# Stick-breaking attention with its products for two query blocks at a time

## Chip, cores and metric

One core of one Trainium2 chip. The metric is device time in microseconds (us), the median of several executions. TensorE does the matrix products, VectorE and ScalarE the elementwise work, GpSimd (POOL) and SyncE (SP) issue most of the transfers.

## What is computed

Two blocks follow each other on one sequence of 1024 tokens of width 1024. The change touches one part of the first block, the stick-breaking attention: 16 heads of 64, query blocks of 128, keys up to the end of the query's own block.

```python
def stick_breaking_attention(q, k, v):
    for i in range(seq // Q_BLOCK):                 # 8 blocks of 128 queries
        ...
        z = jnp.einsum('bhqd,bhkd->bhqk', qb, kb) * inv_sqrt_d
        mask = kpos < qpos
        log_beta = jax.nn.log_sigmoid(z)
        log_1m_beta = jnp.where(mask, log_beta - z, 0.0)
        suffix = lax.cumsum(log_1m_beta, axis=3, reverse=True) - log_1m_beta
        a = jnp.where(mask, jnp.exp(log_beta + suffix), 0.0)
        outs.append(jnp.einsum('bhqk,bhkd->bhqd', a.astype(vb.dtype), vb))
```

The mask is strict: a query doesn't see its own position, so the last key of a query block has weight zero for every query of that block.

## The kernel before

The program is written as one order of instructions for each engine. A planner (class `Sched`, L58) makes this order: it keeps a clock for each engine, prices every instruction in `note` (L153) and lets side tasks (Python generators) put in their instructions when the planned clock has come to the time that they wait for. The main line is a row of projections (`run_q0`, `run_z0`, ... at L2268 on), the attention is a side task. On the chip each engine runs its list in order and waits on semaphores. All instructions are recorded in a helper, so matrix products show L249 and almost everything else L250 in the profile; it is the tile names that tell them apart: `pj` and `pv` projections (operands in a reduced fp32 format, fp32r, split in high and low parts), `z` scores, `ob` or `om`/`be` the weights, `tr` transposes, `aT` transposed weights, `o` the products with the values, `vp` the values.

Stick-breaking runs in two halves of 512 queries (`stick`, L1068). For each head pair `p` (8 of them), query block `i` (4 in a half) and head `h` there is one unit, `work`. At most three units are under way (`crew`, L1035). A unit forms the scores (`z`, L1091), sigmoid of minus and plus the scores on ScalarE (`om` and `be`, L1094), a running product from the last key backwards on VectorE (L1100), and the weights (L1102). This leaves the last key's column of `be` as it was. `turn` (L1009) transposes the weights 128 x 128 at a time on TensorE, four blocks to a PSUM bank, and ScalarE copies them to `aT`. When both heads of a query block are there, the products with the values follow (L1117): for each key block and head one product in full fp32, 64 columns of values as weights, 128 columns of `aT` moving past them. The two heads write to the two halves of the partitions. The last key block takes only 127 rows, which leaves the last key out. A PSUM bank holds the four query blocks of a half; when the third is done the gate `z` is loaded (L1126), after the fourth VectorE multiplies (L1135), and the result stays in SBUF for the output projection if at least ten big buffers are free (L1136) or goes by way of memory.

Big buffers are 34 tiles of 4 KB a partition (`N4`); a task that needs some waits in `room` (L312) until the count allows it. In `stick` a unit with over 512 keys asks for three (`om`, `be`, `aT`) and holds one until the products are done.

The output projection of the first half (`run_bo0`, L2275) begins after the first half's stick-breaking, that of the second half (`run_bo1`, L2283) after projections of the second block.

Of the kernel before, what the change touches and what calls it, by code (L numbers as in the profile page):

```python
# [12 lines left out]
ACTF = mybir.ActivationFunctionType  # L13
# [5 lines left out]
HT = 512  # L19
# [38 lines left out]
class Sched:  # L58
# [94 lines left out]
    def note(self, eng, op, out, args, extra=0.0):  # L153
        ready = self.ready
        names = [a.tensor.name for a in args]
        self.seq += 1
        start = max([self.clk[eng]] + [ready.get(n, 0.0) for n in names])
        o = out.tensor.name
        n = out.free_size()
        lat = 0.1  # L160
        if eng == "pe":
            start = max(start, self.fresh.pop(o, 0.0))
            if op == "transpose":
                d = 0.113 if self.t > 30.0 else 0.213
            elif args[0].dtype == F32R:
                d = n / 2400 if n >= 256 else n / 600
            elif args[0].dtype == BF16:
                d = n / 2400
            elif n == 1:
                d = 0.2 if self.t > 30.0 else 0.37  # L170
            else:
                d = n / 600 if args[0].free_size() == 128 else n / 1070
            d += 0.0026
        elif eng == "act":
            d = n / 1400 + 0.155 + extra
        elif eng == "dve":
            fast = op in ("tensor_scalar", "tensor_copy") and all(a.space == out.space != bass.MemoryType.PSUM
                                                                  for a in args)
            d = n / (1920 if fast else 960) + 0.06
            if op == "reciprocal":  # L180
                d += n / 192
        else:
            d = 1.05 if eng == "pool" else 0.55
            nbytes = n * out.shape[0] * 4
            t = max(self.clk["dma"], start + d) + nbytes / 360e3
            self.clk["dma"] = t
            lat = t + 1.8 - start - d
        self.clk[eng] = start + d
        for nme in names + [o]:
            self.last[nme] = self.seq, max(start + d + lat, self.last.get(nme, (0, 0.0))[1])  # L190
        ready[o] = max(ready.get(o, 0.0), start + d + lat) if eng != "pe" else start + d + lat
        if eng != "pe":
            for nme in names:
                b = self.in_bank.get(nme)
                if b is not None:
                    b[0] = max(b[0] or 0.0, start + d)
# [68 lines left out]
def tile_body(  # L265
# [14 lines left out]
    sch = Sched()  # L280
    ten, sca, vec, syn, pol = (Engine(e, n, sch, plan is None) for e, n in (
        (nc.tensor, "pe"), (nc.scalar, "act"), (nc.vector, "dve"), (nc.sync, "sp"), (nc.gpsimd, "pool")))
    acq = Engine(nc.scalar, "actq", sch, plan is None)
    mm = ten.matmul
    act = sca.activation
# [11 lines left out]
    out = out[0]  # L297
# [10 lines left out]
    def free(n=1):  # L308

        in_use[0] -= n  # L310

    def room(n, hold=0):  # L312

        while in_use[0] + n > N4:
            yield 0.4
        in_use[0] += hold

    def big(shape, dt=F32, name="b", held=False):
        in_use[0] += not held
        return s4.tile([128] + shape, dt, nm(name))  # L320

    def sml(w=HT, dt=F32, name="s"):
        return s2.tile([128, w], dt, nm(name))
# [4 lines left out]
    def bank(name="ps"):  # L328
        return sch.new_bank(lambda n: pp.tile([128, HT], F32, tag=f"bk{n}", name=nm(name)))
# [371 lines left out]
    flags = set()  # L701
# [307 lines left out]
    def turn(src, n):  # L1009

        dst = wide(n * 128, name="aT", held=True)
        for b0 in range(0, n, 4):
            b1 = min(n, b0 + 4)
            yield from sch.a_bank()
            ps = bank("tr")
            for b in range(b0, b1):
                ten.transpose(out=ps[:, (b - b0) * 128:(b - b0 + 1) * 128],
                              in_=src[:, b * 128:(b + 1) * 128], identity=ident)
            sca.copy(out=dst[:, b0 * 128:b1 * 128], in_=ps[:, 0:(b1 - b0) * 128])
        yield dst  # L1020
        return dst

    def fetched(loads, keys, need, fetch, tiles, ahead=1):

        for n, key in enumerate(keys):
            while (need(key) not in flags) or (n > ahead and keys[n - ahead - 1] not in loads["done"]):
                yield 0.5
            yield from room(tiles + (KEEP if n else 0))
            loads[key] = fetch(key)
# [38 lines left out]
    def stick(live, half, width, rho):  # L1068
        nk = (half + 1) * HT
        kv, qs = stick_in[half]  # L1070
        st = {}

        def work(p, i, h):
            yield from arrived(kv, p)
            yield from arrived(qs, p)
            n = i + 1
            w = n * 128
            kk, vt, q = kv[p][0][h], kv[p][1], qs[p][h]
            yield kk, q
            qb = q[:, :, (i % 4) * 128:(i % 4 + 1) * 128]  # L1080
            yield from room(1 if w <= HT else 3, int(w > HT))
            if w <= HT:
                both = big([2, HT], name="ob")
                om, be = both[:, 0, :], both[:, 1, :]
            else:
                om, be = big([D], name="om"), big([D], name="be")
            for c0, c1 in CUTS[n]:
                yield from sch.a_bank()
                ps = bank("z")
                o = ps[:, 0:c1 - c0]  # L1090
                mm(o, lhsT=qb[:, 0, :], rhs=kk[:, c0:c1], start=True, stop=False)  # L1091
                mm(o, lhsT=qb[:, 1, :], rhs=kk[:, c0:c1], start=False, stop=True)
                e = min(c1, w)
                act(out=om[:, c0:e], in_=ps[:, 0:e - c0], func=ACTF.Sigmoid, scale=-1.0)  # L1094
                act(out=be[:, c0:e], in_=ps[:, 0:e - c0], func=ACTF.Sigmoid)
            yield om


            rev = om[:, 0:w][:, ::-1]
            vec.tensor_tensor_scan(out=rev, data0=rev, data1=cst1["begin"][:, D - w:D][:, ::-1], initial=0.0, op0=ALU.mult,  # L1100
                                   op1=ALU.add)
            vec.tensor_tensor(out=be[:, 0:w - 1], in0=be[:, 0:w - 1], in1=om[:, 1:w], op=ALU.mult)  # L1102
            free(w > HT)
            yield be
            aT = yield from turn(be, n)
            free()
            got = st.setdefault((p, i), {})
            got[h] = aT
            if len(got) < 2:
                return  # L1110
            if p not in st:
                yield from sch.a_bank()
            if p not in st:
                st[p] = [bank("o"), 0]
            po = st[p][0]
            yield vt
            for kb in range(n):  # L1117
                r = slice(0, 127 if kb == n - 1 else 128)
                for hh in range(2):
                    mm(po[64 * hh:64 * hh + 64, (i % 4) * 128:(i % 4 + 1) * 128],  # L1120
                       lhsT=vt[r, kb * 128 + 64 * hh:kb * 128 + 64 * hh + 64],
                       rhs=got[hh][r, kb * 128:(kb + 1) * 128], start=kb == 0, stop=kb == n - 1)
            free(2 * (w > HT))
            del st[p, i]
            st[p][1] += 1
            if st[p][1] == 3 and ("z", p, half) in flags:  # L1126
                zs[p, half] = sml(name="zl")
                syn.dma_start(out=zs[p, half], in_=z_d[p, :, hs(half)])
            if st[p][1] == 4:
                o = sml(name="o")  # L1130
                z = zs.get((p, half))
                if z is None:
                    vec.tensor_copy(out=o, in_=po)
                else:
                    vec.tensor_tensor(out=o, in0=po, in1=z, op=ALU.mult)  # L1135
                if z is not None and in_use[0] + R_OB <= N4:  # L1136
                    flags.add(("oB", p, half))
                    sch.spawn(split_to(("oB", p, half), o))
                else:
                    store(o_d[p, :, hs(half)], o)  # L1140
                del kv[p], qs[p], st[p]
                free(3 + 2 * half)
                kv["done"].add(p)
                qs["done"].add(p)

        yield from crew(live, [(p, i, h) for p in range(8) for i in range(4 * half, 4 * half + 4) for h in range(2)],
                        work, width, lambda p, i, h: rho * 0.32 * (i + 1), lambda: flags.add(("stick", half)))
# [1186 lines left out]
```

## Time and profile before

| | us |
|---|---|
| median of 3 runs | 2580.68 (2580.65 to 2581.55) |
| profiled execution | 2582.41 |
| its span | 2580.6 |
| TensorE busy | 2505.5 (97%) |
| weight loads busy | 2057.5 (80%) |
| VectorE busy | 1792.8 (69%) |
| ScalarE busy | 1255.7 (49%) |
| GpSimd busy | 490.0 (19%) |

The mean granted clock of TensorE was 0.991 of its full 2.4 GHz. A group of instructions is a line, an engine and an operation with its tiles, written out<-in. A busy time is the union of the records' times, and records of TensorE overlap and have modelled ends; how often one follows the other is read from their starts.

### The profile page before, as it was taken

Reading aid. Unit: us, or ns where it says so; the run is one execution under the profiler, and the core shown is the slowest. Engines: PE = TensorE matmul, PEld = TensorE weight load, DVE = VectorE, ACT = ScalarE, POOL = GpSimd, SP = SyncE. Lnnn points to the kernel's source line nnn. Section 1 sums busy time; section 2 is a strip of 40 time slices with the busy share of each in tenths; the row PEclk is TensorE's granted clock in tenths of the full one; section 3 lists DMA queues with packets and bytes.
Section 4 is the critical chain, followed back from the end, with each engine's and each line's share of the span. In section 5 each row is a group of like instructions: output and inputs, shape, how many; then the busy total and the mean of one; then the engine's idle time right before and its main releaser. Section 6 shows DMA issues by size and latency. Waiting matters only on the chain.

```text
span 2580.6 us, 38805 instructions
## 1 busy us (share of the span) xinstructions
PE 2505.5 (97%) x13215; PEld 2057.5 (80%) x13215; DVE 1792.8 (69%) x3245; ACT 1255.7 (49%) x2529; POOL 490.0 (19%) x894
## 2 busy tenths in 40 slices
PE   7999999989999899998999999999999899999998
PEld 6888888879877677787888887888888678788887
DVE  7866666777697788986765556774666876677555
ACT  5311112555455677677664353564634634345442
POOL 0012112312101002331211321222222222221000
PEclk9999999999999999999999999999999999999999
DMA  9867869857897665775876978977886987978764
GB/s 283 264 190 201 203 214 280 235 185 249 279 274 222 204 163 157 221 192 140 250 217 160 262 209 261 260 226 220 200 237 217 237 225 235 238 225 252 226 201 130
DMA packets 541726, 570.43 MB, mean 221 GB/s; under 512 B 32910, under 2 KB 410008, under 8 KB 541528
## 3 DMA queue, kind: packets, MB, share of 16 engines
q1 hardware_dynamic: 482644, 381.99, 50.3%
q0 software_dynamic: 56528, 181.75, 25.3%
q10 hardware_dynamic: 2356, 4.21, 0.4%
q8 instruction: 104, 1.70, 0.3%
q14 instruction: 94, 0.77, 0.1%
HBM read 466.90 MB, written 186.91 MB: 253 GB/s over the span
## 4 chain that ended last, share of the span: by engine, by line
PE 65%; DVE 5%; DMA 3%; ACT 2%; issue 2%; SPq 0%; POOL 0%; DVEq 0%; ACTq 0%; POOLq 0%
PE pj L249 53%; PE o L249 4%; PE z L249 4%; PE tr L250 3%; DVE om L250 2%; PE pv L249 1%; DMA wr<-sg_d2g 1%; DVE be L250 1%; DVE wl L250 1%; DMA wr<-in_b_w_out_dram 1%; DVE ob L250 1%; DVE act L250 0%; DVE fa L250 0%; ACT om L250 0%; ACT be L250 0%
## 5 line engine op out<-in xcount | busy, mean ns | idle before, releaser
L249 PE MATMUL pj<-act,wh 128*128 128x512 f32 (+1 forms) x5680 | 1783.0, 395 | 26.2 <-DVE act L250 16.8
L249 PEld LDWEIGHTS pj<-act,wh 128*128 128x128 f32 x5680 | 1046.2, 189 | 256.8 <-DVE act L250 22.9
L249 PE MATMUL pj<-act,wl 128*128 128x512 f32 (+1 forms) x2840 | 1113.7, 392 | 0.0
L249 PEld LDWEIGHTS pj<-act,wl 128*128 128x128 f32 x2840 | 536.2, 189 | 123.1 <-DVE wl L250 1.3
L250 DVE TENSOR_TENSOR wl<-wr,wh 128x512 fp32r<-128x512 f32 x714 | 476.4, 679 | 169.7 <-ACT wh L250 156.2
L250 ACT CAST wh<-wr 128x512 fp32r<-128x512 f32 x714 | 425.8, 617 | 177.6 <-PE pj L249 41.8
L250 POOL COPY paced<-wl 128x1 f32<-128x1 f32 x256 | 114.7, 448 | 881.6 <-DVE wl L250 840.9
L250 ACT COPY aT<-tr 128x512 f32<-128x512 f32 (+3 forms) x272 | 128.7, 501 | 162.0 <-PE tr L250 159.6
L249 PE MATMUL z<-kd,qs 128*128 128x512 f32 (+2 forms) x704 | 166.4, 350 | 1.7 <-DVE o L250 0.7
L250 DVE SCALAR_TENSOR_TENSOR acc<-mw,silu_c,acc 128x512 f32<-128x512 f32 x196 | 146.5, 748 | 2.7 <-DMA mw<-in_a_mod_w_dram 0.3
L249 PEld LDWEIGHTS z<-kd,qs 128*128 128x128 f32 x704 | 113.7, 190 | 19.4 <-issue 7.2
L250 DVE TENSOR_TENSOR_SCAN om<-om,begin 128x640 f32<-128x640 f32 (+3 forms) x64 | 120.6, 1885 | 10.2 <-ACT om L250 10.2
L249 PEld LDWEIGHTS o<-aT,vp 128*64 128x64 f32 (+2 forms) x1440 | 99.9, 149 | 22.8 <-issue 14.5
L249 PE MATMUL o<-aT,vp 128*64 128x128 f32 (+2 forms) x1440 | 116.3, 280 | 0.4 <-ACT aT L250 0.4
L250 ACT COPY u<-pj 128x512 f32<-128x512 f32 x46 | 27.0, 588 | 157.8 <-PE pj L249 80.1
L250 ACT ACTIVATE p<-p,t 128x256 f32<-128x256 f32 (+7 forms) x128 | 81.3, 636 | 20.7 <-DVE t L250 20.5
L250 ACT ACTIVATE sq<-xn 128x512 f32<-128x512 f32 x48 | 30.6, 637 | 110.6 <-DVE xn L250 110.5
L250 ACT ACTIVATE om<-z 128x384 f32<-128x384 f32 (+2 forms) x128 | 69.3, 542 | 22.6 <-PE z L249 19.0
L249 PE MATMUL pj<-wh,act 128*128 128x256 f32 x448 | 79.9, 281 | 0.0
L250 PE MATMUL tr<-ident,be 128*128 128x128 f32 x416 | 61.1, 283 | 18.1 <-DVE be L250 17.7
L250 PEld LDWEIGHTS tr<-ident,be 128*128 128x128 f32 x416 | 47.3, 143 | 32.4 <-DVE be L250 20.7
L250 DVE TENSOR_TENSOR be<-be,om 128x639 f32<-128x639 f32 (+3 forms) x64 | 66.2, 1034 | 6.7 <-ACT sq L250 0.5
(252 smaller groups left out, 2757.5 us busy)
## 6 DMA issues: line engine op xcount, KB each, us to landing
wr<-in_w_in_dram SPq DMA_DIRECT2D x136, 256.0 KB
mw<-in_w_ada_dram SPq DMA_DIRECT2D x96, 256.0 KB
wr<-in_a_w_in_dram SPq DMA_DIRECT2D x80, 256.0 KB
al<-dn_d SPq DMA_DIRECT2D x77, 256.0 KB
wr<-in_w_up_dram SPq DMA_DIRECT2D x66, 256.0 KB
sw_d<-in_w_down_dram POOLq DMA_DIRECT2D x48, 352.0 KB, 5.0
wr<-in_b_w_qz_dram SPq DMA_DIRECT2D x64, 256.0 KB
qs<-q_d SPq DMA_DIRECT2D x64, 256.0 KB
```

Of the source, the lines that this page charges most:

```text
L249: return f(out, *value, **kw)
L250: return f(out=out, **kw)
```

## The change

Two neighbouring query blocks `i0` and `i0 + 1` of a head share their transposed weights: for each key block 256 columns, the first 128 of the one and the last 128 of the other query block. `turn_pair` writes them there. `pair_new` gives the place: for block pair 0 one small tile, for pair 2 one big buffer, for pairs 4 and 6 two big buffers, for each head. The unit of the first block of a pair asks for them (`room`) and the second waits until the first has begun. The products are made once for both heads and both query blocks are there: for each key block one product of 256 columns, and for the last key block, which only the second query block sees, one of 128. The last key's weight is set to zero by a new ScalarE Copy with scale 0 on one column, and the last key block takes all 128 rows. `z` is loaded after the first pair, when two query blocks are done. The planner's price for full-fp32 products is changed too: it was 128/600 us for 128 columns past full weights and 128/1070 past half-width weights, and is 0.213 and 0.108 us there, and for 256 columns 0.233 and 0.116 us.

```diff
@@ -169,7 +169,7 @@
-                d = n / 600 if args[0].free_size() == 128 else n / 1070
+                d = max(n / 1100, 0.213) if args[0].free_size() == 128 else max(n / 2200, 0.108)
@@ -1020,6 +1020,30 @@
+    def pair_tiles(i):
+
+        return (i % 8) // 2 if i < 4 else 2
+
+    def pair_new(i):
+        return [sml(name="aT")] if i == 0 else [big([2 * HT], name="aT", held=True) for _ in range(pair_tiles(i))]
+
+    def pair_block(tiles, kb, j):
+
+        return tiles[kb // 4][:, kb % 4 * 256 + 128 * j:kb % 4 * 256 + 256]
+
+    def turn_pair(src, n, tiles, j):
+
+        for b0 in range(0, n, 4):
+            b1 = min(n, b0 + 4)
+            yield from sch.a_bank()
+            ps = bank("tr")
+            for b in range(b0, b1):
+                ten.transpose(out=ps[:, (b - b0) * 128:(b - b0 + 1) * 128],
+                              in_=src[:, b * 128:(b + 1) * 128], identity=ident)
+            dst = tiles[b0 // 4].rearrange("p (k j q) -> p k j q", j=2, q=128)
+            sca.copy(out=dst[:, 0:b1 - b0, j, :], in_=ps[:, 0:(b1 - b0) * 128].rearrange("p (k q) -> p k q", q=128))
+        yield tiles
@@ -1078,7 +1102,13 @@
-            yield from room(1 if w <= HT else 3, int(w > HT))
+            i0, j = i & ~1, i % 2
+            extra = 0 if j else pair_tiles(i)
+            while j and (p, i0, h) not in st:
+                yield 0.4
+            yield from room((1 if w <= HT else 2) + extra, extra)
+            if not j:
+                st[p, i0, h] = []
@@ -1093,6 +1123,7 @@
+            act(out=be[:, w - 1:w], in_=be[:, w - 1:w], func=ACTF.Copy, scale=0.0)
             yield om
@@ -1102,11 +1133,14 @@
-            aT = yield from turn(be, n)
+            aT = st[p, i0, h]
+            if not aT:
+                aT.extend(pair_new(i0))
+            yield from turn_pair(be, n, aT, j)
             free()
-            got = st.setdefault((p, i), {})
-            got[h] = aT
-            if len(got) < 2:
+            done = st.setdefault((p, i0), [])
+            done.append((h, j))
+            if len(done) < 4:
                 return
@@ -1114,16 +1148,17 @@
-            for kb in range(n):
-                r = slice(0, 127 if kb == n - 1 else 128)
+            got = [st.pop((p, i0, hh)) for hh in range(2)]
+            for kb in range(i0 + 2):
+                j0 = int(kb > i0)
                 for hh in range(2):
-                    mm(po[64 * hh:64 * hh + 64, (i % 4) * 128:(i % 4 + 1) * 128],
-                       lhsT=vt[r, kb * 128 + 64 * hh:kb * 128 + 64 * hh + 64],
-                       rhs=got[hh][r, kb * 128:(kb + 1) * 128], start=kb == 0, stop=kb == n - 1)
-            free(2 * (w > HT))
-            del st[p, i]
-            st[p][1] += 1
-            if st[p][1] == 3 and ("z", p, half) in flags:
+                    mm(po[64 * hh:64 * hh + 64, (i0 % 4 + j0) * 128:(i0 % 4 + 2) * 128],
+                       lhsT=vt[:, kb * 128 + 64 * hh:kb * 128 + 64 * hh + 64],
+                       rhs=pair_block(got[hh], kb, j0), start=kb == 0, stop=kb > i0)
+            free(2 * pair_tiles(i0))
+            del st[p, i0]
+            st[p][1] += 2
+            if st[p][1] == 2 and ("z", p, half) in flags:
```

## Rows read from the trace of the kernel before

**Rows 1.** The page, busy us of each engine with its share of the span.
```profile
PE 2505.5 (97%) x13215; PEld 2057.5 (80%) x13215; DVE 1792.8 (69%) x3245; ACT 1255.7 (49%) x2529; POOL 490.0 (19%) x894
```

**Rows 2.** Windows: stretch, length, busy us of PE, PEld, DVE, ACT, POOL; clock; DMA.
```profile
690.00:880.00 190.00, 187.10 (x1129) 144.17 (x1127) 152.04 (x252) 107.48 (x256) 20.01 (x37) 1.00 0.86 258
880.00:1210.00 330.00, 303.34 (x2242) 252.65 (x2243) 277.80 (x332) 241.89 (x532) 67.59 (x94) 0.97 0.63 173
```

**Rows 3.** Waits of TensorE, 690 to 1210 us: total, times, longest.
```profile
PE tr L250 <- DVE be L250: 17.7, 20, 3.7
```

**Rows 4.** Lines by form: count, busy us, mean ns of one, idle before.
```profile
L249 PE MATMUL o<-aT,vp 128*64 128x128 f32 x896 | 63.3, 283 | 0.4 <-ACT aT L250 0.4
L249 PE MATMUL o<-aT,vp 127*64 127x128 f32 x256 | 26.2, 278 | 0.0
L249 PEld LDWEIGHTS o<-aT,vp 128*64 128x64 f32 x896 | 49.4, 139 | 18.1 <-issue 13.0 <-ACT ob L250 2.9 <-ACT aT L250 0.7
L249 PEld LDWEIGHTS o<-aT,vp 128*128 128x128 f32 x288 | 36.4, 191 | 2.2
```

**Rows 5.** Time line of TensorE, 863 to 865 us: start, length, operation, count.
```profile
864.41 0.66 PE L249 MATMUL o<-aT,vp 128*64 128x128 f32 x8
865.01 0.55 PE L250 MATMUL tr<-ident,ob 128*128 128x128 f32 x3
```

**Rows 6.** Time line of TensorE, 1102 to 1105 us.
```profile
1102.04 0.63 PE L249 MATMUL pj<-act,wh 128*128 128x512 f32 x2
1102.50 0.39 PE L249 MATMUL pj<-act,wl 128*128 128x512 f32 x1
1102.82 1.53 PE L249 MATMUL o<-aT,vp 128*64 128x128 f32 x24
1104.29 0.76 PE L250 MATMUL tr<-ident,be 128*128 128x128 f32 x5
```

**Rows 7.** Time line of TensorE, 1206 us: 256 columns in the reduced format.
```profile
1206.19 0.29 PE L249 MATMUL pv<-wh,act 128*128 128x256 f32 x1
1206.31 0.28 PE L249 MATMUL pv<-wl,act 128*128 128x256 f32 x1
```

**Rows 8.** Time line of TensorE, 993 us: full fp32 with 264 columns.
```profile
992.76 0.71 PE L249 MATMUL row<-row,ones 1*128 1x264 f32 x2
993.40 0.55 PE L249 MATMUL o<-aT,vp 128*64 128x128 f32 x6
```

**Rows 9.** Time line of TensorE, 40 us: full fp32 with one column.
```profile
39.75 0.95 PE L249 MATMUL sm<-ones,acc 128*128 128x1 f32 x8
40.56 0.71 PE L249 MATMUL pj<-act,wh 128*128 128x512 f32 x2
```

**Rows 10.** Lines, 690 to 1210 us: VectorE's scan and ScalarE's smallest operation.
```profile
L250 DVE TENSOR_TENSOR_SCAN om<-om,begin 128x640 f32<-128x640 f32 (+3 forms) x64 | 120.6, 1885 | 10.2 <-ACT om L250 10.2
L250 ACT ACTIVATE t<-t 128x2 f32<-128x2 f32 (+1 forms) x9 | 1.8, 199 | 0.1
```

**Rows 11.** Time line of all engines, end of the first half; idle time and releaser in brackets.
```profile
879.83 0.69 DVE L250 TENSOR_TENSOR o<-o,zl 128x512 f32<-128x512 f32 x1 [6.95 <-DMA zl<-z_d]
...
884.78 1.33 PE L250 MATMUL tr<-ident,be 128*128 128x128 f32 x5 [3.71 <-DVE be L250]
```

**Rows 12.** The chain that ended last within 866 to 900 us: start, length, what.
```profile
872.86 7.67 DMA wr<-in_b_w_out_dram
```

**Rows 13.** Tile `o`: count, ns min/median/max, first and last start.
```profile
L250 DVE TENSOR_TENSOR o<-o,zl x13: 685/692/692, 761.0 to 1209.0; 128x512 f32<-128x512 f32 x13
L250 POOL DMA_DIRECT2D o_d<-o x10: 539/542/582, 718.5 to 1154.6; - x10
...
L250 DVE COPY o<-o x3: 683/691/692, 717.5 to 997.2; 128x512 f32<-128x512 f32 x3
```

**Rows 14.** Time lines of TensorE (1205 us on) and SP's queue (1322 us on).
```profile
1206.99 1.97 PE L249 MATMUL o<-aT,vp 128*64 128x128 f32 x32
...
1325.80 7.53 SPq L250 DMA_DIRECT2D wr<-in_b_w_out_dram  x5
```

## Prediction

> **What bounds the kernel now.** I began with the busy times on the page: TensorE is busy 97% of the span [rows 1]. Busy time of TensorE is a model, so I next looked at the stretch that the change touches, stick-breaking, in two windows [rows 2]: the first half of the queries (690 to 880 us) and the second (880 to 1210 us). In the first, TensorE is busy for 187.1 of 190 us and VectorE for 152.0. In the second TensorE leaves 26.7 of 330 us unused and VectorE is busy for 277.8, 84%. Who waits for whom comes third: between 690 and 1210 us the longest wait of TensorE is for VectorE's `be`, the finished weights that are transposed next, 17.7 us in 20 pieces [rows 3]. So the first half is bound by TensorE, and time taken from it there is time gained. In the second half some of it may only lengthen the wait for VectorE. Last I went down to single products in the time line, because the price of one product decides this case.
>
> **The products, before.** For one key block the two heads' products run side by side in the two halves of the array's columns. One product of full fp32 is two records, so four records stand for one key block. There are 896 + 256 = 1152 of them [rows 4], which is 288 key blocks (8 head pairs times 1 to 8 blocks) in 64 groups, one for each pair and query block. A group of 8 records lasts 0.60 us until the next operation starts [rows 5], one of 24 lasts 1.47 us [rows 6]. The difference is 0.87 us for 16 records, 0.054 us each: 0.218 us for a key block, 0.109 us for two records side by side. What is left over, 0.60 - 8 x 0.054 = 0.165 us, is fixed for each group. Ahead of the group there is more: the last projection record starts 0.32 us before it, while two of them take 0.46 us when projections follow one another [rows 6]. That is 0.32 - 0.23 = 0.09 us. **A group thus costs 0.25 us beyond its records**, for going over to half-width columns and back.
>
> **What 256 columns cost.** The change turns 128 + 128 columns past two loads into 256 past one. Per head pair 1 + 3 + 5 + 7 = 16 key blocks go to 256 columns and 4 stay at 128. Over 8 pairs these are 128 and 32 key blocks, so 256 and 64 steps of two records side by side, instead of 576 steps of 128 columns. It saves streaming only if the 0.109 us of a step is the load of the values and not the 128 columns. No full-fp32 product of 256 columns past half-width weights stands in this trace, so I bound it. From below: a record of the reduced fp32 format with 256 columns starts 0.12 us before the next [rows 7]. From above: the two `row` records, full fp32 with 264 columns (from one partition), take 0.64 us until the next operation, 0.32 each [rows 8].
>
> Two rows point in opposite directions. Eight full-fp32 records with one moving column and a load of 128 weight columns take 0.81 us, 0.10 each [rows 9]: there the load sets the pace, and by analogy it could set it in the products. But in the products the load is of 64 columns for each head and takes 139 ns against 191 ns for 128 columns [rows 4], so it is shorter by 52 ns and the step is still 0.109 us. And the 0.64 us of `row` take apart cleanly: 0.10 us for the first load, which nothing hides [rows 9], 0.09 us for going over to half-width products behind them, and 0.45 us for two records, 0.225 us each. That is 264 columns at 0.109 us per 128 columns. I take the value in proportion to the columns, 0.218 us for a step of 256, because `row` is the only full-fp32 row with so many columns. Streaming then gains nothing: 256 x (0.218 - 2 x 0.109) = 0.
>
> The Trainium skill has a sentence for each side. FP8 and Floating Point Precision, TensorE Precision Notes, gives true fp32 four passes through the array; with two records for a product that is two passes in each, and the rows of `row` agree. Perfetto Trace Analysis, Engine Utilization, gives the low-high fp32 mode half of the array's output rate, which would be one pass for each record; by it the sum would be that of rival B below.
>
> **The sum.**
> - Groups: 64 become 32, because one group now serves two query blocks. 32 x 0.25 = 8 us of TensorE time less, 4 in each half. The first half is bound by TensorE and gives all 4. Of the second I count 2, because TensorE's spare time there is larger than the saving [rows 2] and it waits for VectorE [rows 3]; the bounds are 0 and 4.
> - Streaming: 0. Between its bounds it would be -25 us (0.12 a step) and +26 us (0.32).
> - The new one-column Copy on ScalarE, 128 of them (16 heads, 8 query blocks). The nearest row is an operation on two columns, 199 ns [rows 10], so 128 x 0.2 = 26 us of ScalarE, which is busy for 107.5 + 241.9 = 349 of the 520 us [rows 2]. It stands behind the sigmoids of its block, and the scan on VectorE, which needs `om` alone, takes 1.9 us on average meanwhile [rows 10]. I count nothing. Without that cover each block's chain would be 0.2 us longer; what queues behind it on ScalarE is the next weight split.
> - The copies out of the transposes keep number and size; only the place that they write to changes. Nothing.
> - The last group of the first half now holds two query blocks, four key blocks instead of one query block's four of 128: 3 x 0.218 us more behind the last transpose, +0.7 us. The projection of the output waits for it, so it counts. Elsewhere the products of a pair's first block now wait for the second block's weights, but nothing except the multiplication by `z` at the end of a half waits for them.
> - The load of `z` is issued one query block earlier, by SP, ahead of loads of `q` and weights. In the trace VectorE stands still for 6.95 us at 879.8 us for the last of these loads, and TensorE then waits 3.71 us [rows 11]. A gain of up to 3.7 us offers itself, but ScalarE was at that time held up until 880.5 us by a weight load of 7.67 us [rows 12], which comes next after this one. I count nothing, and -3.7 as the bound.
> - The planner's new price for a 256-column product is 256/2200 + 0.003 = 0.119 us, so 0.237 for both heads; by my reading it is 0.436, so it thinks 128 x 0.2 = 25 us of TensorE time away and lays the side work out accordingly. Projections then stand rather too early in the order than too late, which costs waiting in neither engine that I can point to: 0, with 3 us either way.
>
> Sum: -4 - 2 + 0.7 = -5.3 us, rounded to **-6 us** because the bounds on `z` and on the second half lie below. The profiled execution took 2582.41 us (span 2580.6 us), 1.7 us over the median of 2580.68. Taken from the first it gives 2576.4; for the median I forecast **2574.7 us**.
>
> **The rivals.**
> A is the forecast: columns set the price, half of the group switches are saved, 2574.7 us (2569 to 2581 with the bounds that are not streaming).
> B: the load sets the price, and a step of 256 columns takes 0.12 us. For it stand the one-column records [rows 9], against it the halved load [rows 4] and `row` [rows 8]. It would save 0.098 x 64 = 6.3 us in the first half, and 0.098 x 192 = 18.8 us in the second, of which half to all arrive: 2574.7 - 6.3 - 9.4 to 18.8 = 2550 to 2559, say 2555 us.
> C, the slower side: the pool of 34 big buffers. Two heads' pairs hold four transposed buffers in the second half until all four units are done, where each query block held two. In the trace 13 outputs were multiplied by `z` in place and 10 outputs went by way of memory, only 3 of these for lack of `z`: so at 7 of 13 ends over 24 of the 34 were in use [rows 13]. If the three units at work fall to two, the second half's 329 us (880 to 1209 us, where the last group of products ends) become 494 and end at 1374 us, 48 us after the second output projection's weights were first fetched (1325.8 us) [rows 14]. Below 117 us of lengthening it costs nothing, since nothing waits for this end before that. 2574.7 + 48 = 2623 at worst, 2600 for half of it.
> D: the order of the second half takes the rest back: its 2 us go, and VectorE's and ScalarE's extra waits take 1 to 3 us more. 2578 to 2581, say 2579 us.
>
> **How the numbers follow.** A 0.58, B 0.15, C 0.12, D 0.15. What can be told from no change is about 0.2%, 5.2 us: below 2575.5 counts as faster, above 2585.8 as slower. A straddles the lower line; I give it 0.34 faster and 0.24 same. B is faster, D is same, C is slower (0.12). Faster 0.49, same 0.39, slower 0.12. The range 2553 to 2584 takes in A with its bounds, D, and the greater part of B; C and the fast end of B are left out, somewhat under 0.2.
>
> **What would show it.** In the profile after: 640 records of this product, of them 512 with 256 columns; such records side by side start 0.21 to 0.22 us apart (A) or 0.12 us (B). 32 groups, with 0.09 us ahead and 0.165 us in each, as before. TensorE's unused time between 880 and 1210 us stays near 27 us (A) or grows by what the products gave up (D). The 128 Copies take about 0.2 us each and nobody is released by them. If C holds, the last group of the second half ends after 1325 us. I am wrong if a step of 256 columns takes clearly less than 0.21 us, if the groups' switches are not halved, or if the stretch before 690 or after 1400 us changes by more than the whole.

## The result and the profile after

| | before | after |
|---|---|---|
| median of 4 executions each, on the same chip, us | 2581.11 | 2601.80 |
| profiled execution, us (span) | 2582.41 (2580.6) | 2603.45 (2601.6) |
| mean granted clock of TensorE | 0.991 | 0.986 |

The ratio is 1.0073 with a 95% interval of 1.0051 to 1.0094: 19 us slower (0.0073 x 2581; the medians differ by 20.7), where 6 us faster was forecast. The time lies 18 us above the upper end of the range.

**The products do what was forecast.** From the page-wide list of groups by shape, then from TensorE's time line of the second half (start, duration, records, then idle time and its releaser), kernel after:

```profile
L249 PE MATMUL o<-aT,vp 128*64 128x256 f32 x512 | 65.5, 397 | 0.0
L249 PE MATMUL o<-aT,vp 128*64 128x128 f32 x128 | 13.3, 277 | 0.0
L250 ACT ACTIVATE be<-be 128x1 f32<-128x1 f32 x64 | 13.0, 203 | 2.0
L250 ACT ACTIVATE ob<-ob 128x1 f32<-128x1 f32 x64 | 13.0, 203 | 2.0
```
```profile
1103.28 2.60 PE L249 MATMUL o<-aT,vp 128*64 128x256 f32 x24
1105.80 1.08 PE L249 MATMUL z<-kd,qs 128*128 128x512 f32 x4
...
1126.53 3.46 PE L249 MATMUL o<-aT,vp 128*64 128x256 f32 x32
1129.92 0.33 PE L250 MATMUL tr<-ident,be 128*128 128x128 f32 x1
```

512 and 128 records, as counted beforehand against 1152 in [rows 4]. The group of 32 lasts 3.39 us until the next operation starts, that of 24 lasts 2.52; the difference of 0.87 us is eight records of 256 columns, four steps of 0.2175 us. Twice a step of 128 columns is 0.218 [rows 5, 6]. What is left of the larger group is 3.39 - 14 x 0.2175 - 2 x 0.109 = 0.13 us, not far from the 0.165 us of a group before. The Copy takes 203 ns, as assumed.

**What went wrong stands in the windows.** Columns as in [rows 2]; first the two stretches of [rows 2], then the end of the first half and the main line's last wait for an attention, kernel after:

```profile
690.00:880.00 190.00, 182.11 (x982) 139.60 (x982) 152.43 (x254) 118.82 (x325) 21.07 (x39) 1.00 0.88 261
880.00:1210.00 330.00, 296.32 (x1771) 237.95 (x1769) 255.14 (x335) 227.88 (x537) 63.33 (x91) 0.94 0.59 163
860.00:940.00 80.00, 65.63 (x350) 50.03 (x349) 51.43 (x61) 46.60 (x118) 1.76 (x4) 0.87 0.46 136
1840.00:1920.00 80.00, 76.09 (x366) 62.68 (x365) 47.11 (x94) 41.75 (x70) 20.15 (x37) 0.98 0.88 218
```
The last two for the kernel before:
```profile
860.00:940.00 80.00, 72.19 (x516) 58.67 (x517) 65.98 (x67) 57.62 (x129) 3.25 (x6) 0.96 0.62 184
1840.00:1920.00 80.00, 80.00 (x375) 65.66 (x374) 50.46 (x92) 35.73 (x61) 18.68 (x37) 1.00 0.87 235
```

In the second half (880 to 1210 us) TensorE's unused time grows from 26.7 to 33.7 us and its clock falls from 0.97 to 0.94. VectorE, 84% busy there before, does 22.7 us less in the same stretch, and ScalarE 14.0 less. So none of these engines became busier there: units of work come later. The stretch then runs on. The groups of VectorE's multiplication by `z` and of the second attention's output statistics, by tile (duration ns, then first and last start), after and then before:

```profile
L250 DVE TENSOR_TENSOR o<-o,zl x14: 685/691/692, 767.7 to 1311.8; 128x512 f32<-128x512 f32 x14
L250 ACT ACTIVATE sq<-o x8: 600/604/605, 1332.2 to 1886.4; 128x512 f32<-128x512 f32 x8
```
```profile
L250 DVE TENSOR_TENSOR o<-o,zl x13: 685/692/692, 761.0 to 1209.0; 128x512 f32<-128x512 f32 x13
L250 ACT ACTIVATE sq<-o x8: 602/604/607, 1278.9 to 1856.5; 128x512 f32<-128x512 f32 x8
```

The second half's stick-breaking ends at 1311.8 us instead of 1209.0, 103 us later, and what follows it, the second block's attention, at 1886.4 instead of 1856.5. The main line falls behind along the way. Counted in projection records, the 3600th starts 0.1 us later than before (925 us), the 4800th 18.6 us (1395 us), the 6600th 25.7 us (1883 us), the 9450th 21.3 us (2556 us). The 2400th (591 us), ahead of all that the change touches, is already 3.2 us late in this execution, so a few us of such counts say nothing. The line thus loses ground at two places, up to 1400 us and around 1885 us. On the way to the first it seemed to gain: at 1210 us the projections were 42.6 us ahead, because TensorE had not done the attention's share, and that share came after.

### The profile page after: what moved, and what is told of

Same layout as the page of the kernel before. It is cut to its first block, busy times and chain, and to the rows that moved or that the text cites. A ratio compares the mean times of both kernels' runs of the same rounds, so it can differ in the third digit from the quotient of the medians.

```text
span 2601.6 us, 37805 instructions
## 1 busy us (share of the span) xinstructions
PE 2508.6 (96%) x12703; PEld 2048.0 (79%) x12703; DVE 1791.9 (69%) x3244; ACT 1287.6 (49%) x2665; POOL 488.9 (19%) x892
## 4 chain that ended last, share of the span: by engine, by line
PE 51%; DVE 4%; ACT 2%; DMA 1%; issue 1%; SPq 0%; DVEq 0%; ACTq 0%
PE pj L249 42%; PE o L249 3%; PE z L249 2%; PE tr L250 2%; PE pv L249 1%; DVE om L250 1%; DMA wr<-in_w_up_dram 1%; DVE p L250 1%; DVE wl L250 1%; ACT om L250 0%; ACT be L250 0%; DVE fa L250 0%; DVE t L250 0%; DMA wr<-sg_d0g 0%; DMA wr<-sg_d3a 0%
## 5 line engine op out<-in xcount | busy, mean ns | idle before, releaser
L250 DVE TENSOR_TENSOR_SCAN om<-om,begin 128x640 f32<-128x640 f32 (+3 forms) x64 | 120.6, 1885 | 26.3 <-ACT om L250 26.2
L249 PE MATMUL o<-aT,vp 128*64 128x256 f32 (+2 forms) x928 | 109.4, 343 | 0.3 <-ACT aT L250 0.2
L249 PEld LDWEIGHTS o<-aT,vp 128*64 128x64 f32 (+1 forms) x928 | 81.2, 156 | 32.5 <-issue 7.3
```

The source lines that it names most:

```text
L249: return f(out, *value, **kw)
L250: return f(out=out, **kw)
```

## Experiments: which half, which part

All are compared with the kernel before on the same chip; "end" is the last multiplication by `z` of the second half.

**e1, e2: the planner's price alone.** In e1 the kernel before has the new price line, in e2 the changed kernel the old one.

```diff
-                d = n / 600 if args[0].free_size() == 128 else n / 1070
+                d = max(n / 1100, 0.213) if args[0].free_size() == 128 else max(n / 2200, 0.108)
```


> The kernel before with nothing but the planner's new price for full-fp32 products (0.213 and 0.108 us at 128 columns in place of 128/600 and 128/1070); no product changes. Pool theory (the second half's units and fetches wait for big buffers, because two heads' pairs hold four of the 34): 2581 +-5 us, end of the second half's stick-breaking at 1209 +-15 us. Price theory (the planner's wrong prices disturb the order): about 2595 to 2602 us. Structure theory (products that wait for four units): 2581 us.

> The changed kernel with the old price line in the planner (a 256-column product past half-width weights at 256/1070 = 0.239 us, close to the 0.21 to 0.22 us that the trace of after shows). Pool theory: still slow, 2602 +-8 us, the second half's last products after 1290 us. Price theory: 2576 +-6 us. Structure theory: 2602 us.

e1: 2586.21 us, ratio 1.0009 (1.0000 to 1.0018). e2: 2599.57 us, 1.0064 (1.0049 to 1.0079), end 1312.0. By the medians the price is worth 2 or 3 us; without it the changed kernel still loses 0.64%, so it is not the cause.

**e3, e4: pairs in one half only.** The changed lines are kept for one half, the old ones for the other; e4 has `PAIRED = (1,)`. Both have the new price.

```diff
+    PAIRED = (0,)
...
+            if half in PAIRED:
```


> Pairs in the first half alone (blocks 0 to 3, where a pair holds at most one big buffer a head); the second half as before, without the Copy; new price. Pool theory: the first half's gain stays and the second half loses nothing: 2573 to 2578 us, last products near 1209 us. Price theory: 2590 to 2600 us. Structure theory (half of the pairs, half of the loss): about 2590 us.

> Pairs in the second half alone (blocks 4 to 7, two big buffers a head); the first half as before; new price. Pool theory: all of the loss and none of the first half's gain: 2602 to 2612 us, last products after 1290 us. Price theory: 2590 to 2600 us. Structure theory: about 2590 us.

e3: 2583.81 us, 1.0001 (0.9991 to 1.0011), end 1210.0. e4: 2593.44 us, 1.0039 (1.0024 to 1.0054), end 1280.5. The first half gains nothing, although its groups are halved; the second half alone loses 10 us. Together they lose 19: the two are not a sum. Both miss what the theory of the buffer pool alone expected (2573 to 2578 and 2602 to 2612 us).

**e9: without the Copy.** The changed kernel; the last key's weight is not set to zero, so that part of the computation is left out.

```diff
-            act(out=be[:, w - 1:w], in_=be[:, w - 1:w], func=ACTF.Copy, scale=0.0)
```


> The changed kernel without the one-column Copy on ScalarE (the last key's weight is then not set to zero; 128 operations of 203 ns, 26 us of ScalarE, are left out). Theory that the Copy lengthens every unit's chain: the second half ends 10 us or more earlier and the time falls to 2590 us or less. Pool theory: 2601 +-4 us, end of the second half near 1310 us.

2595.66 us, 1.0046 (1.0031 to 1.0061), end 1272.7. The Copy is worth about 6 us by the medians, with intervals that overlap, and 39 us of the end. The time lies between the two theories' ranges.

## Experiments: why the first half gives nothing

**e10, e11: a wait moved.** Late in the main line, projections of the feed-forward (`run_up0`, pieces 0 to `M_BR`) stand before the wait for the second attention's second half. The edit puts one more piece in front; e10 has the pairs in the first half only, e11 is the kernel before.

```diff
-M_BR = 5
-M_WO = 6
+M_BR = 6
+M_WO = 7
```


> Pairs in the first half alone, and one more step of the up projection put ahead of the wait for the second attention (M_BR 6, M_WO 7 in place of 5 and 6). Gate theory (in e3 the main line is 5.8 us ahead at 1800 us and loses 7.4 us at 1865 us, where it waits for the end of the second attention): that wait goes, what TensorE loses between 1840 and 1920 us falls from 8.2 to about 1 us, and the time is 2574 to 2580 us. If the saved time was lost elsewhere: 2584 us as e3.

> The kernel before with the same step ahead of the same wait: control for e10. Before loses 0.9 us between 1840 and 1920 us, so nothing is to be had there: 2581 to 2588 us by the gate theory. If it gains as much as e10, the gain of e10 is not that of the pairs.

**e10 takes 2577.93 us, ratio 0.9977 (0.9967 to 0.9987): faster than both kernels.** e11 takes 2595.8 us, 1.0045 (1.0030 to 1.0060), so it is not the edit by itself. This control missed its range (2581 to 2588 us), and why it is slow stays open: at the 6900th projection (1953 us) it is level with the kernel before, at the 8100th (2252 us) 12.9 us behind, where e10 loses nothing. The window of the wait, e3 and then e10:

```profile
1840.00:1920.00 80.00, 76.09 (x343) 62.03 (x342) 49.95 (x91) 35.18 (x60) 16.42 (x31) 0.96 0.84 212
```
```profile
1840.00:1920.00 80.00, 80.00 (x374) 65.67 (x373) 51.73 (x95) 39.99 (x66) 18.96 (x34) 1.00 0.87 231
```

In e3 TensorE came to this point 5.8 us earlier than before (the 6300th projection), but the attention's last statistics were taken at 1861.1 us instead of 1856.5. TensorE waited ahead of two small products of these statistics, and its granted clock was half for 6.8 us from 1863.8 us on. Its waits in this window in e3 (total, times, longest):

```profile
PE rb L250 <- DVE t L250: 2.3, 1, 2.3
PE sm L250 <- ACT sq L250: 1.4, 1, 1.4
```

With the up to 3.4 us that half clock costs in 6.8, all the gain was gone. Before, this wait does not exist. With the wait a piece later TensorE is busy for all 80 us at full clock, and the gain arrives.

**e5, e6: the wait at the first half's end moved.** Two more pieces of the `z` projection ahead of the wait for the first half's stick-breaking, with the pairs in the first half (e5) and in the kernel before (e6).

```diff
-N_Z = 2
+N_Z = 4
```


> Pairs in the first half alone, and two more of the gate projections (48 products of 512 columns, 11 us of TensorE) put ahead of the wait for the first half's end (N_Z 4 in place of 2). Gate theory (the first half's TensorE time was saved, about 4 us, but the main line then waits at the end of stick-breaking's first half for a chain through ScalarE and VectorE that ends no earlier): 2574 to 2579 us, and what TensorE loses between 860 and 940 us falls from 23 to about 15 us. Theory that the pairs themselves slow the units at the boundary: 2584 us as in e3, the loss moves with them.

> The kernel before with the same two projections ahead of the wait (N_Z 4), nothing else: control for e5. Gate theory: there the main line and the chain end together (878 and 880 us), so moving 11 us of work ahead of the wait delays what comes after it: 2581 to 2588 us. If it is faster by as much as e5, the gain of e5 is not that of the pairs.

e5: 2585.89 us, 1.0008 (0.9998 to 1.0017). e6: 2591.82 us, 1.0030 (1.0019 to 1.0040). With this order the pairs of the first half are worth 6 us, e5 against e6, but the order itself costs more than that, and both lie above their ranges (e5 2574 to 2579, e6 2581 to 2588 us). In e5 the projections were 20.8 us ahead at 998 us and 0.4 us behind at 1064 us: the time was given back at the next wait.

## Experiments: why the second half is late

**e13: held, but not paired.** The kernel before; in the second half the products of two neighbouring query blocks wait for all four units and are then made with 128 columns, block after block.

```diff
+            ii = i & ~1 if half else i
...
-            if len(got) < 2:
+            if len(got) < (4 if half else 2):
...
+            for iq in range(ii, ii + 1 + half):
...
-            free(2 * (w > HT))
+            free(2 * (1 + half) * (w > HT))
```


> The kernel before; only in the second half the products of two neighbouring query blocks wait until all four units (two query blocks, two heads) are done, and are then made one query block after the other with 128 columns, as before; the four transposed buffers are held until then. z is loaded when the first two query blocks are done. No 256-column product, no Copy, the old price. Theory (holding): the second half's last multiplication by z comes at 1250 to 1320 us instead of 1209, TensorE's unused time grows in 940 to 1080 us and around 1880 us, and the time is 2589 to 2600 us, near the kernel with pairs in the second half alone (2593). Rival (the wide products themselves, their order of writing, the Copy): the end stays within 10 us of 1209 and the time within 4 us of before.

2603.07 us, 1.0073 (1.0058 to 1.0088), end 1245.5.

```profile
L250 DVE TENSOR_TENSOR o<-o,zl x13: 684/691/693, 762.9 to 1245.5; 128x512 f32<-128x512 f32 x13
```

No wide product, no Copy, no new price, and the time of the changed kernel. The time is 3 us over the theory's range and the end 4.5 us below it; the rival (4 us, an end within 10 us) is out. Making the products wait for four units, and holding the transposed weights until then, is enough for a loss of 19 us. With wide products, the Copy and the new price on top (e4) it is 10 us: together these give some back. Not all of the 19 us need be the holding's own. In its profiled execution e13 falls 14 us behind between the 2400th and the 6900th projection (591 and 1953 us) and 9 us more by the 8100th, in the stretch where e11 loses 12.5 us with no holding at all. So a rival was not tested and may hold for a part: that a changed order costs time by itself, as it does in e6 and e11 (8 and 12 us without a pair), though not in e17.

**e8: two buffers fewer, nothing held.**

```diff
-N4 = 34
+N4 = 32
```


> The kernel before with 32 big buffers in place of 34, nothing else: what two buffers fewer cost by themselves. Pool theory: the second half's end goes from 1209 to 1270 us or later, 2590 to 2602 us. Structure theory: 2581 to 2586 us, end near 1209 us.

2626.94 us, 1.0165 (1.0150 to 1.0180), end 1259.8. That is 25 us over the upper end of the range. The window of the late wait shows where it goes:

```profile
1840.00:1920.00 80.00, 48.06 (x244) 42.17 (x243) 42.73 (x125) 40.21 (x71) 11.18 (x23) 0.77 0.52 129
```

TensorE stands idle for 32 of these 80 us. The pool is so tight that two of 34 buffers delay the second half's end by 51 us. But the pool serves the whole program: the second attention's last statistics come at 1913.1 us, 57 us later, and at the 6300th projection, before that wait, TensorE is 26.8 us ahead of the kernel before. So e8 shows that buffers are short, not what their lack in stick-breaking alone costs.

**e7, e12: one big buffer for each head of a pair,** with key blocks from the fifth on in small tiles; e7 in the changed kernel, e12 with pairs in the second half only.

```diff
-        return (i % 8) // 2 if i < 4 else 2
+        return int(i > 0)
...
+        return t + [sml(name="aT") for _ in range(1 if i == 0 else max(0, i // 2 - 1))]
```


> The changed kernel, but the transposed weights of key blocks 4 to 7 in small tiles from the other pool: a head's pair holds one big buffer where it held two, as many as a query block held before; one ScalarE copy more where a bank is split in two. Pool theory: the end of the second half's stick-breaking comes back from 1312 to 1215 +-20 us and the time to 2586 +-6 us (the loss at the first half's end stays). Structure theory: end at 1290 to 1312 us, 2600 us.

> Pairs in the second half alone with one big buffer a head and small tiles for key blocks 4 to 7: e4 (2593.4 us, end at 1280 us) with fewer big buffers. Pool theory: the end comes back to 1209 to 1240 us and the time to 2582 to 2588 us. Structure theory (products and buffers that wait for four units, however large): 2591 to 2596 us, end near 1280 us.

e7: 2592.64 us, 1.0032 (1.0019 to 1.0045), end 1262.7. e12: 2592.51 us, 1.0038 (1.0026 to 1.0049), end 1260.4. Half of the delay of the end goes and 9 us of the time in e7; against e4, e12 gains nothing that can be told. With half of the big buffers for each later pair, the theory of the pool expected the end at 1195 to 1235 (e7) and 1209 to 1240 us (e12), and both missed it.

**e16, e17, e18: the loads.** Loads of a head pair's keys and values, and of its queries, need buffers of their own (three and two) and wait in `fetched` (L1023) until `KEEP` = 7 more are free. Issues of the keys' loads from 880 us on, by tile (the last two numbers are first and last start): after, before, e13.

```profile
L250 SPq DMA_DIRECT2D kd<-k_d x12: 338/440/3739, 965.5 to 1210.0; - x12
```
```profile
L250 SPq DMA_DIRECT2D kd<-k_d x12: 319/338/455, 932.9 to 1109.3; - x12
```
```profile
L250 SPq DMA_DIRECT2D kd<-k_d x12: 320/403/655, 946.7 to 1169.6; - x12
```

The third head pair's keys are asked for 33 us later and the last pair's 101 us later, about the delay of the end. The edit lets the second half's loads go with three more buffers free (`keep` is 3 there); e16 is the changed kernel, e17 the kernel before, e18 the kernel of e7.

```diff
-            yield from room(tiles + (KEEP if n else 0))
+            yield from room(tiles + (keep if n else 0))
```


> The changed kernel; the loads of keys, values and queries of the second half go as soon as their own buffers and 3 more are free, instead of 7 more. Theory (the loads are what holds the second half up): the third head pair's keys are issued near 935 us instead of 965 and the last near 1110 to 1150 instead of 1210, the second half ends at 1215 to 1260 instead of 1312, and the time is 2586 to 2594 us. Rival (the units themselves lack the buffers, or wait for the products of four units): loads come earlier, the second half still ends after 1280 us and the time is 2596 to 2606.

> Control: the kernel before with the same edit. Theory: its loads were not late (a gap of at most some us), so the second half's end stays within 10 us of 1209 and the time within 3 us of before. Rival: the margin of seven matters in itself, and the time moves by over 5 us to either side.

> The changed kernel with one big buffer for each head of a pair (key blocks from the fifth on in small tiles) and the loads' margin of 3. Theory (both are ways of the same lack): second half's end 1215 to 1250 us, time 2582 to 2590. Rival: as the lean kernel alone, end 1255 to 1275, time 2590 to 2595.

e16: 2594.13 us, 1.0042 (1.0025 to 1.0058), end 1282.6. e17: 2585.12 us, 1.0002 (0.9993 to 1.0012), end 1212.7. e18: 2592.88 us, 1.0032 (1.0022 to 1.0042), end 1238.1. In e16 the last keys are asked for at 1152.6 us, 57 us earlier than in the changed kernel, and the end comes 29 us earlier. So late loads are a part of the delay, some 8 us of time by the medians, with intervals that just overlap. In e16 its end lies in the rival's range and its time at the edge of the theory's: neither is the whole. In e18 the end is nearly back (29 us late) and the time did not follow.

What else delays the units: VectorE's waits from 890 us on (total, times, longest; after up to 1320 us, before up to 1210 us).

```profile
DVE o L250 <- PE o L249: 34.7, 7, 10.4
```
```profile
DVE o L250 <- PE o L249: 9.8, 5, 3.4
```

VectorE carries out its list in order, and the multiplication by `z` of a head pair stands in it ahead of other units' scans. It now waits for a group of two query blocks. The longest of these waits shows three things in a row, in the time lines of VectorE and of TensorE, kernel after:

```profile
976.62 0.68 DVE L250 TENSOR_TENSOR wl<-wr,wh 128x512 fp32r<-128x512 f32 x1
987.65 0.69 DVE L250 TENSOR_TENSOR o<-o,zl 128x512 f32<-128x512 f32 x1 [10.35 <-PE o L249]
988.26 0.68 DVE L250 TENSOR_TENSOR sq<-sq,sq 128x512 f32<-128x512 f32 x1
```
```profile
976.05 0.40 PE L249 MATMUL pj<-act,wl 128*128 128x512 f32 x1
980.33 1.40 PE L249 MATMUL z<-kd,qs 128*128 128x384 f32 x4 [3.88 <-issue]
981.53 1.05 PE L249 MATMUL pj<-act,wh 128*128 128x512 f32 x2
982.39 0.63 PE L249 MATMUL pj<-act,wl 128*128 128x512 f32 x1
982.95 4.66 PE L249 MATMUL o<-aT,vp 128*64 128x256 f32 x32
987.53 1.57 PE L249 MATMUL z<-kd,qs 128*128 128x384 f32 x8
```

TensorE stops for 3.88 us ahead of the next head pair's scores; the profile names no engine, and that pair's keys and queries had been asked for from 965 us on, so I take the wait to be for them. It goes on at half clock (0.50 from 980.4 to 982.9 us), and the group of 32 records takes 4.58 us instead of 3.39. VectorE, 84% busy in this half before, stands still for 10.35 us meanwhile. The sum of such waits does not by itself tell the loss: e17 has 18.8 us of them at the time of the kernel before, e13 20.0 us.

How much of the delay is units without a buffer and how much is such waits was not separated; both come with waiting for four units. The traces show a longer way of each unit and fewer units at once. Over the second half's first 48 units, six head pairs, a unit takes 9.7 us before and 10.9 after from its first score product to its last transpose, and 1.95 and 1.82 units are between the two on average: one every 5.0 us before, every 6.0 after. In e13 it is mostly the number (10.0 us, 1.82 units), in e7 with fewer big buffers the length (10.7 us, 1.96 units).

**e14, e15: the later wait with the whole change.** M_BR 6 and M_WO 7 as in e10, in the changed kernel and in the kernel of e7.

> The changed kernel with M_BR 6 and M_WO 7 instead of 5 and 6: the second output projection's part and the wait for the second attention come one piece later in the main line. Theory (a part of the loss lies at the main line's waits for the attention): the 7 us that TensorE lost between 1840 and 1920 us fall to about 1, and the time is 2592 to 2596 us; what is lost at 860 to 1080 us stays. Rival (with the second half 103 us late, the later wait only moves the loss behind 1920 us, as it did in the kernel before with the same edit): 2598 to 2610 us.

> The changed kernel with one big buffer for each head of a pair (key blocks from the fifth on in small tiles) and with M_BR 6 and M_WO 7. Theory: both losses go partly, 2583 to 2589 us, since the lean kernel took 2592.6 and the later wait was worth 6 us with pairs in the first half alone. Rival: the later wait gives nothing here, 2590 to 2596 us.

e14: 2603.27 us, 1.0069 (1.0052 to 1.0086), in the rival's range; TensorE is busy for all of 1840 to 1920 us, and the time is lost after it: the 6600th projection starts 17.7 us late, the 8100th 22.7. e15: 2591.27 us, 1.0021 (1.0011 to 1.0031), in the rival's range, 1 us below e7. The later wait paid in e10 alone. A second half that ends late goes with no gain (e14, e15), but one on time is not enough: e11 has it and loses 12 us.

## Why the prediction was wrong, step by step

The forecast counted -4 us in the first half, -2 in the second, and nothing for two query blocks that wait for each other. Measured are 0 for the first half alone (e3), +10 for the second alone (e4), and +19 for both.

- **Streaming, 0: right.** 0.2175 us a step against 0.218 taken. Rival B (0.12) is out. FP8 and Floating Point Precision, TensorE Precision Notes, in the Trainium skill, gives true fp32 four passes, and the trace agrees: two steps make a product, 0.435 us for 256 columns, where one record of the reduced format has 0.12 [rows 7], 3.6 times as much.
- **Groups, 32 x 0.25 = 8 us: right as TensorE's own time.** 32 groups are left. In the first half (670 to 860 us) the time from each TensorE record to the next, beyond that shape's usual spacing at full clock, sums to 15.0 us before, 11.0 after and 10.4 in e3. The -4 is there.
- **"The first half is bound by TensorE and gives all 4": this step failed first.** It was read from the stretch's busy share [rows 2], and up to 860 us it held. In the last 20 us of the stretch TensorE leaves 4.4 us unused where it left 0.1, and over the stretch 7.9 where it left 2.9. Its waits from 690 to 880 us, after and then before:

```profile
PE tr L250 <- DVE ob L250: 7.1, 11, 1.2
```
```profile
PE tr L250 <- DVE ob L250: 2.5, 6, 0.9
```

  So the stretch now ends in waits for the stick-breaking chain, and a later one waits for the second attention. Neither chain became shorter: the first half's last multiplication by `z` moved from 879.8 [rows 11] to 886.6 us. What TensorE saves ahead of a wait that another chain ends is not saved there. With pairs in the first half alone the later wait is the one that takes it: e3 is 5.9 us ahead of the kernel before at 1395 us (the 4800th projection) and 1.6 us behind at 1883 us (the 6600th), and e10 gives the 6 us back when that wait is moved.
- **The last group, +0.7 us: mis-sized.** It is 3.90 us long, where the steps above give 6 x 0.2175 + 2 x 0.109 + 0.15 = 1.67, as the same group of the head pair before takes at 866.9 us. It ran at half clock, which makes 3.34, and within it the loads of weights waited 0.45 us for `aT`. TensorE's time line, after:

```profile
876.27 0.52 PE L250 MATMUL tr<-ident,ob 128*128 128x128 f32 x3 [0.51 <-DVE ob L250]
877.71 0.55 PE L250 MATMUL tr<-ident,ob 128*128 128x128 f32 x3 [0.92 <-DVE ob L250]
...
879.73 1.08 PE L250 MATMUL tr<-ident,ob 128*128 128x128 f32 x4 [1.01 <-DVE ob L250]
881.57 1.12 PE L250 MATMUL tr<-ident,ob 128*128 128x128 f32 x4 [0.76 <-DVE ob L250]
882.61 3.96 PE L249 MATMUL o<-aT,vp 128*64 128x256 f32 x16
886.51 1.73 PE L249 MATMUL z<-kd,qs 128*128 128x384 f32 x9
```

  Four waits for `ob` of 0.5 to 1.0 us stand in the 7 us before it; the clock granted from 880 to 887 us is 0.54. In the whole run 75.5 us are at 1.2 GHz, before 50.4: at half speed that is worth up to 12.5 us, which no term of the sum held.
- **"Nothing except the multiplication by `z` waits for them": true, and the mistake.** That one instruction stands in order on VectorE ahead of other units (34.7 us of waiting against 9.8), and the weights that wait hold their buffers. How much each costs is not shown.
- **The second half, -2, between 0 and -4: wrong sign, and the step that cost most.** e4 shows +10, and e13 +19 for the waiting and holding without wide products. The term for it stood at nothing.
- **The Copy, 0: probably mis-sized.** e9 gives about 6 us for 128 of them, 26 us of ScalarE, with intervals that overlap. What it holds up on ScalarE was not traced.
- **The price, 0 with 3 either way: right** within what e1 and e2 tell. **The load of `z`, 0,** was not tested by itself.
- **Rival C came nearest, in part by luck.** That four held buffers delay the second half is borne out (e13, half of the delay in e7), and its "half of it", 2600 us, is near 2601.8. But that number came from three units at work falling to two, where the traces have 1.95 falling to 1.82; its sign, an end after 1325 us, did not come; and it made lateness free up to 117 us, because only the output projection's weights seemed to wait. The end came 103 us later, at 1311.8 us, still before the 1325.8 us of [rows 14], and it cost all the same. I had counted units in need of buffers, and not the loads, which need nine or ten free ones, nor the second block's attention, which shares VectorE and ScalarE and whose place in TensorE's order is fixed.

How a late end turns into lost time stays open: e13's end, 37 us late, goes with a loss of 19 us, e4's, 71 us late, with 10, and e18's, 29 us late, with 8.

## What to carry to other kernels

That an engine is 98% busy in a stretch does not tell that its saving reaches the end: a later wait that another chain ends can take it. Look up the chain that ends each later wait before counting the gain. A fusion that makes results wait for each other holds their buffers for longer: list everything that asks for the same pool, the loads too, and what stands behind the fused operation on each in-order engine. If a half-sized version of the change has no such cost (here the first half, whose buffers fit), make that, and then try to move the wait that it runs into: e10 is 0.2% faster than the kernel before. Try it with a control, since the same move cost 0.45% in the kernel before (e11).

## What was not expected of the hardware

Here work right behind a stop of TensorE ran at half clock and took longer. Around the stop of 3.88 us at 976 us the clock granted was 1.2 GHz from 978.6 to 985.4 us, and a group that takes 3.39 us at full clock took 4.58. On ScalarE an operation on one column takes 203 ns, where the sigmoids of 256 to 512 columns beside it take 393 to 656 ns: a correction of one column is not cheap, though it touches almost nothing.
